# A two-layer encoder on one core: a third pair of split weight buffers, the attention bias masked by VectorE, and the softmax maximum kept with its sign turned

## The chip, the core and the metric

One core of a Trainium2 chip runs the whole program in one launch. The time is the device time in microseconds (us) of one execution; the medians are over several executions. Engines: PE is TensorE (matrix products), DVE is VectorE, ACT is ScalarE, POOL is GpSimd, SP is SyncE (it issues DMAs here). PEld is TensorE's weight load, which overlaps its products.

## The reference, cut to what is computed

Two layers on 256 rows of 1024, everything in float32. A layer is a mixer and a gated feed-forward.

```python
h = rms_norm(x, n1);  proj = h @ w_in_l                      # 1024 -> 2560
# a: 4 heads of neighbourhood attention, q and k normed per head, bias rpb per offset
s = einsum(q, k[idx]) * scale + bias;  out_a = softmax(s) @ v[idx]
# d: 6 heads, dilated windows (three patterns), partial rotary on q and k
# c: 6 query heads on 2 key/value heads, full attention, axial rotary on q and k
mix = concat(rms_norm(out_a), rms_norm(out_d), rms_norm(out_c))
x = x + mix @ w_out_l                                        # 1024 -> 1024
g, u = split(rms_norm(x, n2) @ w_gu)                         # 1024 -> 2 x 2816
g = conv3(g)                                                 # along the rows
x = x + (gelu(g) * u) @ w_dn                                 # 2816 -> 1024
```

## The kernel before, in words

**Products in split form.** A float32 weight is split into a high part (ScalarE rounds it, `wp_hi`) and a low part (VectorE subtracts, `wp_lo`), and so are the activations; each product is three faster ones (`mm3`). Weights come in units of up to 2048 columns for each of 128 partitions, in the order of use: `units_of` lists 18 for the mixer and then, for each of 11 feed-forward steps, a gate unit G, an up unit U and a down unit D. A unit lands in one of `RAWS` raw buffers, is split into one of `PARTS` pairs of buffers, and is used by TensorE. `unit()` asks, when unit i is wanted, for the loads up to i + AHEAD + RAWS - PARTS and for the splits up to i + AHEAD. Split instructions work on 384 to 1024 columns.

**Order.** Nothing is issued as written. `Plan` records each operation with what it must follow, and `order()` then gives each engine a fixed queue: again and again it takes the operation that can start earliest by its own costs (`cost`, and an estimate of a DMA's landing), with the place in the program (plus a shift, `later`) breaking ties. A buffer of a tag goes to tiles in the order of the program. Each engine then works through its queue in order, and waits where an operand is not there yet. An operation without operands to wait for may thus move far ahead of its place in the program.

**The mixer.** TensorE's projections and output projections are a filler (`Weave`) between the steps of the 16 heads: six of group d, six of c, four of a. For each two heads `scores` makes scores in PSUM (tile `psw`), `softens` does the softmax (VectorE the bias, the maximum `mx` and its negation `nm`; ScalarE the exponential and the scaling by `rs`), `turn` transposes and splits (`ch`, `cl`), `weigh` multiplies with the values. `prep_d`, `prep_c` and `prep_a` norm and rotate q and k (`z`, `sw`): the sums of squares come from ScalarE or VectorE, GpSimd makes their inverse roots (`small_ms`, `small_rstd`), VectorE or ScalarE scales. The rotation's tables (`cd`, `sd`, `cc`, `sc`, each for q and k) are GpSimd products of constants with a gain, made in `tables_d` and `tables_c` within the layer.

**The bias of group a.** `na_load` loads a few rows of `rpb`, `na_repeat` (GpSimd) scales them by 8 and copies them wide into `nab`, which goes to a scratch in DRAM; `na_diagonals` loads it back along diagonals, 448 KB in each of two DMAs; `na_bias_mask` (GpSimd, three additions of 576 columns) adds the mask. Layer 0 does this in its mixer; for layer 1 the three first steps stand in layer 0's feed-forward at the steps 2, 3 and 4 (`NA_STEPS`), and the mask in layer 1's mixer, but the order puts each where its operands and its buffer are first free: layer 1's copy runs at 110 us, its diagonal loads are issued at 121 us and its mask runs from 129 us, all at the end of layer 0's mixer. Layer 1's tables run at 32 to 57 us.

**From the mixer to the feed-forward.** The last output projections add to `xs` (`const_x`), ScalarE squares, TensorE transposes `xs`, ScalarE and VectorE scale and split it (`act_hT`), then G and U units follow.

The program's recording helper stands at line 393, so nearly every row of the profile has L393; the tiles' names tell the rows apart.

Of the kernel before, what the change touches and what calls it, by code (L numbers as in the profile page):

```python
# [11 lines left out]
F32 = mybir.dt.float32  # L12
# [6 lines left out]
P = 128  # L19
# [22 lines left out]
RAWS, PARTS, AHEAD, CHUNK = 4, 2, 2, 512  # L42
# [174 lines left out]
class Plan:  # L217
    def __init__(self, tc):
        self.tc, self.ops, self.shift, self.burst, self.bursts = tc, [], 0, None, {}
# [13 lines left out]
    @contextmanager  # L233
    def together(self):

        self.burst = len(self.bursts)
        self.bursts[self.burst] = []
        yield
        self.burst = None

    def add(self, engine, method, args, kw):
# [39 lines left out]
        for v in outs:  # L281
            v.tile.writes.append((i, v.footprint()))
        o.before.discard(i)
# [152 lines left out]
def encoder_kernel(  # L436
# [269 lines left out]
    def na_repeat(l):  # L706
        rows_ = nabs[l].rearrange("p r c -> p (r c)")[:NR]
        nc.gpsimd.tensor_scalar(nabs["few"], nabs["few"], ISCALE, None, ALU.mult)
# [7 lines left out]
    def na_diagonals(l):  # L716
        scr = nabs["scr"]
        for i in range(2):
# [3 lines left out]
            )  # L722

    load(0)
    for l in range(DEPTH):
# [81 lines left out]


        def tables_d(which, g):
            cd = act.tile([P, NT, HD], F32, tag=f"cd{which}", name=f"cd{which}{l}", bufs=1)  # L810
            sd = act.tile([P, NT, 16], F32, tag=f"sd{which}", name=f"sd{which}{l}", bufs=1)
            b = lambda v: v.unsqueeze(1).to_broadcast([P, NT, v.shape[1]])
            nc.gpsimd.tensor_tensor(cd, rot[:, :, 0:64], b(g[:, l, 1]), op=ALU.mult)
            for i in range(2):
                o, n = (8 * i, 8 * (1 - i)), 8
                nc.gpsimd.tensor_tensor(
                    sd[:, :, o[0] : o[0] + n],
                    rot[:, :, 64 + o[0] : 64 + o[0] + n],
                    b(g[:, l, 1, o[1] : o[1] + n]),
                    op=ALU.mult,  # L820
                )
            return cd, sd

        def tables_c(which, g):
            cc = act.tile([P, NT, HD], F32, tag=f"cc{which}", name=f"cc{which}{l}", bufs=1)
            sc = act.tile([P, NT, HD], F32, tag=f"sc{which}", name=f"sc{which}{l}", bufs=1)
            b = lambda v: v.unsqueeze(1).to_broadcast([P, NT, v.shape[1]])
            nc.gpsimd.tensor_tensor(cc, rot[:, :, 80:144], b(g[:, l, 2]), op=ALU.mult)
            for i in range(4):
                o, n = (16 * i, 16 * (i ^ 1)), 16  # L830
                nc.gpsimd.tensor_tensor(
                    sc[:, :, o[0] : o[0] + n],
# [544 lines left out]
```

## Time and profile before

| | |
|---|---|
| median of 3 executions | 625.4 us (625.36 to 627.85) |
| the profiled execution | 626.0 us, its span 624.2 us |
| PE busy | 608.7 us, 98% |
| DVE busy | 490.3 us, 79% |
| ACT busy | 430.6 us, 69% |
| POOL busy | 83.3 us, 13% |
| layer 0: mixer, feed-forward | about 0 to 126 us, 126 to 317 us |
| layer 1: mixer, feed-forward | about 317 to 432 us, 432 to 624 us |
| bytes moved | 104.66 MB, mean 168 GB/s |

Busy time is the union of an engine's instructions in the profile. A product's end is modelled, so a busy PE can still hide gaps of some tenths of a microsecond; where a row shows PE idle, it is. The clock granted to TensorE was full in all stages.

### The profile page before, as it was taken

How to read it: one execution, taken by the hardware profiler on the slowest of the kernel's cores; microseconds unless marked ns; L12 is line 12 of the kernel's file. 1: busy time of each engine (PE TensorE's matmuls, PEld its weight loads, DVE VectorE, ACT ScalarE, POOL GpSimd, SP SyncE). 2: the span in 40 equal slices, each digit the busy share in tenths (PEclk: the TensorE clock that was granted, in tenths of full speed). 3: DMA queues.
4: the chain of work that ended last, by engine and by line, in shares of the span. 5: the costliest groups of instructions: out<-in, count | busy, mean ns of one | idle time of the engine just before them, and what ended most of it. 6: DMA issues, size and time to landing. Idle time of an engine off the chain costs nothing.

```text
span 624.2 us, 9846 instructions
## 1 busy us (share of the span) xinstructions
PE 608.7 (98%) x3496; PEld 525.0 (84%) x3496; DVE 490.3 (79%) x1026; ACT 430.6 (69%) x1064; POOL 83.3 (13%) x131
## 2 busy tenths in 40 slices
PE   8999999989999999999999999998999999999997
PEld 6998888778888888888899979786888888888885
DVE  4889889798777777777867798978877777877775
ACT  6887998677655655565588799888765655566552
POOL 2764231340000000000023210312000000000000
PEclk9999999999999999999999999999999999999999
DMA  8794312866555555555444632043565655555511
GB/s 279 262 287 154 102 40 96 249 154 213 189 177 178 199 202 202 179 172 173 153 145 154 225 102 85 34 138 136 202 207 199 202 188 170 187 199 188 170 49 67
DMA packets 81345, 104.66 MB, mean 168 GB/s; under 512 B 9464, under 2 KB 68952, under 8 KB 81296
## 3 DMA queue, kind: packets, MB, share of 16 engines
q1 hardware_dynamic: 80720, 103.51, 51.0%
q8 instruction: 27, 0.44, 0.3%
q10 hardware_dynamic: 576, 0.53, 0.3%
q14 instruction: 22, 0.18, 0.1%
HBM read 102.54 MB, written 1.49 MB: 167 GB/s over the span
## 4 chain that ended last, share of the span: by engine, by line
PE 86%; ACT 4%; DVE 4%; DMA 3%; POOL 1%; issue 1%; SPq 0%; ACTq 0%; POOLq 0%; DVEq 0%
PE psw_w L393 47%; PE psa_a L393 39%; ACT act_s2k L393 2%; DMA act_nab<-dram_scr 1%; DVE wp_lo L393 1%; DMA dram_scr<-act_nab 1%; DVE act_s2k L393 1%; POOL small_rstd L393 1%; DVE act_hT L393 1%; DMA act_s2k<-in_norm_g_dram 1%; POOL act_nab L393 0%; ACT L393 0%; ACT wp_hi L393 0%; DVE const_x L393 0%; DVE act_z L393 0%
## 5 line engine op out<-in xcount | busy, mean ns | idle before, releaser
L393 DVE TENSOR_TENSOR wp_lo<-wp_raw,wp_hi 128x512 fp32r<-128x512 f32 (+2 forms) x348 | 248.3, 742 | 50.9 <-ACT wp_hi L393 49.1
L393 PE MATMUL psw_w<-act_hT,wp_hi 128*128 128x512 f32 x704 | 247.4, 396 | 4.7 <-DVE act_hT L393 4.7
L393 ACT CAST wp_hi<-wp_raw 128x512 fp32r<-128x512 f32 (+2 forms) x348 | 213.7, 658 | 25.1 <-PE psw_w L393 15.6
L393 PE MATMUL psw_w<-act_hT,wp_lo 128*128 128x256 f32 x704 | 195.7, 279 | 0.0
L393 PEld LDWEIGHTS psw_w<-act_hT,wp_hi 128*128 128x128 f32 x704 | 131.8, 188 | 36.8 <-DVE act_hT L393 5.9
L393 PEld LDWEIGHTS psw_w<-act_hT,wp_lo 128*128 128x128 f32 x704 | 132.6, 188 | 1.1
L393 PE MATMUL psa_a<-wp_hi,act_hT 128*128 128x384 f32 (+2 forms) x448 | 114.9, 335 | 0.0
L393 ACT COPY act_s2k<-psw_w 128x256 f32<-128x256 f32 x88 | 32.3, 372 | 81.1 <-PE psw_w L393 81.1
L393 PEld LDWEIGHTS psa_a<-wp_hi,act_hT 128*128 128x128 f32 x448 | 78.6, 190 | 2.3
L393 PE MATMUL psa_a<-wp_lo,act_hT 128*128 128x384 f32 (+2 forms) x224 | 74.6, 334 | 0.0
L393 PE MATMUL psa_a<-wp_lo,act_ch 128*128 128x512 f32 x176 | 69.5, 395 | 0.0
L393 PE MATMUL psa_a<-wp_hi,act_ch 128*128 128x512 f32 x176 | 69.4, 394 | 0.0
L393 PE MATMUL psa_a<-wp_hi,act_cl 128*128 128x512 f32 x176 | 66.2, 395 | 0.2 <-DVE act_cl L393 0.2
L393 DVE TENSOR_TENSOR act_s2k<-psw_w,act_s2k 128x256 f32<-128x256 f32 x88 | 36.8, 422 | 30.6 <-ACT act_s2k L393 30.0
L393 PEld LDWEIGHTS psa_a<-wp_lo,act_hT 128*128 128x128 f32 x224 | 42.5, 190 | 2.1 <-DVE wp_lo L393 1.0
L393 PEld LDWEIGHTS psa_a<-wp_hi,act_cl 128*128 128x128 f32 x176 | 33.2, 188 | 8.3 <-DVE act_cl L393 0.6
L393 PEld LDWEIGHTS psa_a<-wp_hi,act_ch 128*128 128x128 f32 x176 | 33.1, 188 | 7.7
L393 PEld LDWEIGHTS psa_a<-wp_lo,act_ch 128*128 128x128 f32 x176 | 33.1, 188 | 6.9
L393 DVE SCALAR_TENSOR_TENSOR act_s2k<-act_s2k,act_cw,act_s2k 128x255 f32<-128x255 f32 x88 | 36.7, 476 | 1.4 <-ACT act_s2k L393 1.3
L393 ACT ACTIVATE act_s2k<-act_s2k,act_cw 128x256 f32<-128x256 f32 x44 | 24.1, 595 | 13.3 <-DVE act_s2k L393 13.3
L393 POOL TENSOR_TENSOR small_rstd<-small_ms,const_mh 128x6 f32<-128x6 f32 (+2 forms) x26 | 31.3, 1203 | 2.1
L393 ACT ACTIVATE act_s2k<-act_s2k,small_rs 128x256 f32<-128x256 f32 x64 | 28.8, 506 | 3.3 <-DVE small_rs L393 3.3
(110 smaller groups left out, 764.0 us busy)
## 6 DMA issues: line engine op xcount, KB each, us to landing
wp_raw<-in_w_gate_up_dram SPq DMA_DIRECT2D x44, 1024.0 KB, 5.0
wp_raw<-in_w_down_dram SPq DMA_DIRECT2D x22, 1024.0 KB, 4.8
wp_raw<-in_w_in_dram SPq DMA_DIRECT2D x14, 768.0 KB, 4.8
wp_raw<-in_w_in_dram SPq DMA_DIRECT2D x8, 1024.0 KB, 5.5
wp_raw<-in_w_out_dram SPq DMA_DIRECT2D x8, 768.0 KB
wp_raw<-in_w_out_dram SPq DMA_DIRECT2D x4, 512.0 KB, 3.7
act_nab<-dram_scr SPq DMA_DIRECT2D x4, 448.0 KB, 6.7
out_dram<-const_x SPq DMA_DIRECT2D x4, 256.0 KB, 2.0
```

Of the source, the lines that this page charges most:

```text
L393: getattr(o.engine.real, o.method)(*map(real, o.args), **{k: real(v) for k, v in o.kw.items()})
```

## The change

Constants: three raw buffers for four, three split pairs for two, splits asked for three units ahead instead of two. The planner gets `not_before(engine)`: what is recorded inside follows, in the order, the last operation recorded so far for that engine. With it the three bias steps of layer 1 stand behind the last weight load asked for, and layer 1's rotation tables are made in layer 0's feed-forward at step 4, behind the last of the bias's GpSimd work. The bias's scaling on GpSimd goes; mask and scaling are one VectorE operation (`scalar_tensor_tensor`, three in a layer). In the softmax, a head with bias gets minus the score and its minimum, without bias the maximum with its sign turned; both write `nm` themselves, and the negation goes. For group c the score's scale moves into the gain of q (one more GpSimd operation a layer).

```diff
-RAWS, PARTS, AHEAD, CHUNK = 4, 2, 2, 512
+RAWS, PARTS, AHEAD, CHUNK = 3, 3, 3, 512
...
+    @contextmanager
+    def not_before(self, engine):
+        self.behind = max(i for i, o in enumerate(self.ops) if o.engine.name == engine)
+        yield
+        self.behind = None
...
+        if self.behind is not None:
+            o.before.add(self.behind)
...
     def na_repeat(l):
-        nc.gpsimd.tensor_scalar(nabs["few"], nabs["few"], ISCALE, None, ALU.mult)
...
+    def tables_c(l, which):
+        g = gains_of[which][:, l, 2]
+        if which == "q":
+            nc.gpsimd.tensor_scalar(g, g, SCALE, None, ALU.mult)
...
+    def tables_of(l):
+        for which in "qk":
+            tables["d" + which, l] = tables_d(l, which)
+        for which in "qk":
+            tables["c" + which, l] = tables_c(l, which)
...
                         nc.vector.tensor_tensor_reduce(
-                            sb[:, t], sps[t], bias[t], SCALE, -3e38, ALU.add, ALU.max, mx[:, t : t + 1]
+                            sb[:, t], sps[t], bias[t], -SCALE, 3e38, ALU.add, ALU.min, nm[:, t : t + 1]
                         )
-                    nc.vector.tensor_scalar_mul(nm, mx, -1.0)
                     for t in range(NT):
                         nc.scalar.activation(
-                            p[:, t], sb[:, t], AF.Exp, bias=nm[:, t : t + 1], accum_out=rs[:, t : t + 1]
+                            p[:, t], sb[:, t], AF.Exp, bias=nm[:, t : t + 1], scale=-1.0,
+                            accum_out=rs[:, t : t + 1],
                         )
                 else:
                     for t in range(NT):
-                        nc.vector.reduce_max(mx[:, t : t + 1], sps[t], axis=AX.X)
-                    nc.vector.tensor_scalar_mul(nm, mx, -SCALE)
+                        nc.vector.reduce_max(nm[:, t : t + 1], sps[t], axis=AX.X, negate=True)
...
         def na_bias_mask():
             for i in range(1, NR, 9):
                 nv = nabs[l][:, i : i + 9]
-                nc.gpsimd.tensor_tensor(
-                    nv, nv, na_mask.unsqueeze(1).to_broadcast([P, 9, GRID_W]), op=ALU.add
+                nc.vector.scalar_tensor_tensor(
+                    nv, nv, ISCALE, na_mask.unsqueeze(1).to_broadcast([P, 9, GRID_W]), ALU.mult, ALU.add
                 )
...
             if kind == "G" and l + 1 < DEPTH and s in NA_STEPS:
-                NA_STEPS[s](l + 1)
+                with nc.not_before("SP"):
+                    NA_STEPS[s](l + 1)
+            if kind == "G" and l + 1 < DEPTH and s == 4:
+                with nc.not_before("POOL"):
+                    tables_of(l + 1)
```

More of the change, by code (lines that the diff above doesn't have):

```diff
@@ L218, in __init__ @@
     def __init__(self, tc):
-        self.tc, self.ops, self.shift, self.burst, self.bursts = tc, [], 0, None, {}
+        self.tc, self.ops, self.shift, self.burst, self.bursts, self.behind = tc, [], 0, None, {}, None
         for name, short in (("tensor", "PE"), ("scalar", "ACT"), ("vector", "DVE"), ("gpsimd", "POOL"), ("sync", "SP")):
@@ L722, in na_diagonals, with tables_d @@
             )
+    def tables_d(l, which):
+        cd = act.tile([P, NT, HD], F32, tag=f"cd{which}", name=f"cd{which}{l}", bufs=1)
+        sd = act.tile([P, NT, 16], F32, tag=f"sd{which}", name=f"sd{which}{l}", bufs=1)
+        b = lambda v: v.unsqueeze(1).to_broadcast([P, NT, v.shape[1]])
+        nc.gpsimd.tensor_tensor(cd, gains_of["rot"][:, :, 0:64], b(gains_of[which][:, l, 1]), op=ALU.mult)
+        for i in range(2):
+            o, n = (8 * i, 8 * (1 - i)), 8
+            nc.gpsimd.tensor_tensor(
+                sd[:, :, o[0] : o[0] + n],
+                gains_of["rot"][:, :, 64 + o[0] : 64 + o[0] + n],
+                b(gains_of[which][:, l, 1, o[1] : o[1] + n]),
+                op=ALU.mult,
+            )
+        return cd, sd
+    def tables_c(l, which):
+        g = gains_of[which][:, l, 2]
+        if which == "q":
+            nc.gpsimd.tensor_scalar(g, g, SCALE, None, ALU.mult)
+        cc = act.tile([P, NT, HD], F32, tag=f"cc{which}", name=f"cc{which}{l}", bufs=1)
+        sc = act.tile([P, NT, HD], F32, tag=f"sc{which}", name=f"sc{which}{l}", bufs=1)
+        b = lambda v: v.unsqueeze(1).to_broadcast([P, NT, v.shape[1]])
+        nc.gpsimd.tensor_tensor(cc, gains_of["rot"][:, :, 80:144], b(g), op=ALU.mult)
+        for i in range(4):
+            o, n = (16 * i, 16 * (i ^ 1)), 16
+            nc.gpsimd.tensor_tensor(
+                sc[:, :, o[0] : o[0] + n],
+                gains_of["rot"][:, :, 144 + o[0] : 144 + o[0] + n],
+                b(g[:, o[1] : o[1] + n]),
+                op=ALU.mult,
+            )
+        return cc, sc
+    gains_of, tables = {}, {}
+    def tables_of(l):
[3 more added lines that the diff above has]
+            tables["c" + which, l] = tables_c(l, which)
     load(0)
@@ L806, in encoder_kernel @@
             gk = gk.rearrange("p (l a d) -> p l a d", l=DEPTH, d=HD)
[L809 to L815, printed above, removed]
-                nc.gpsimd.tensor_tensor(
[L817 to L832, printed above, removed]
-                    rot[:, :, 144 + o[0] : 144 + o[0] + n],
-                    b(g[:, l, 2, o[1] : o[1] + n]),
-                    op=ALU.mult,
-                )
-            return cc, sc
+            gains_of.update(q=gq, k=gk, rot=rot)
         def normed(ps, nh, t, name):
@@ L946, in softens @@
                 nm = small.tile([P, NT], F32, tag="nm", name=f"nm_{name}")
-                mx = small.tile([P, NT], F32, tag="mx", name=f"mx_{name}")
                 rs = small.tile([P, NT], F32, tag="rs", name=f"rs_{name}")
@@ L1030, in prep_d @@
         def prep_d(which, g):
-            cd, sd = tables_d(which, g)
+            if ("d" + which, l) not in tables:
+                tables["d" + which, l] = tables_d(l, which)
+            cd, sd = tables["d" + which, l]
             for t in range(NT):
@@ L1041, in prep_c @@
         def prep_c(which, g):
-            cc, sc = tables_c(which, g)
+            if ("c" + which, l) not in tables:
+                tables["c" + which, l] = tables_c(l, which)
+            cc, sc = tables["c" + which, l]
             nh = H_GQ if which == "q" else H_GKV
```

4 lines of the change are left out of this document (1 added, 3 removed).

## The prediction, made before the changed kernel ran

> **What bounds the kernel now.** I read the summary first, then busy time by stretches of 10 us, then TensorE's idle time and who ended it, then the order of time around those places.
>
> ```profile
> span 624.2 us, 9846 instructions
> PE 608.7 (98%) x3496; PEld 525.0 (84%) x3496; DVE 490.3 (79%) x1026; ACT 430.6 (69%) x1064; POOL 83.3 (13%) x131
> core 0: us, PE busy (x) PEld busy (x) DVE busy (x) ACT busy (x) POOL busy (x), PEclk, DMA share, GB/s
> 0.00:10.00 10.00, 7.89 (x34) 6.00 (x35) 3.15 (x8) 5.39 (x12) 2.76 (x11) 1.00 0.80 257
> 50.00:60.00 10.00, 8.88 (x64) 7.68 (x64) 10.00 (x30) 7.05 (x19) 4.93 (x7) 1.00 0.38 125
> 110.00:120.00 10.00, 8.69 (x47) 6.70 (x46) 8.23 (x17) 7.58 (x20) 4.08 (x4) 1.00 0.75 244
> 120.00:130.00 10.00, 9.66 (x53) 7.93 (x53) 8.40 (x17) 7.51 (x19) 2.06 (x4) 1.00 0.95 192
> 130.00:140.00 10.00, 8.06 (x50) 6.95 (x49) 10.00 (x16) 5.81 (x13) 5.95 (x6) 1.00 0.56 178
> 170.03:186.70 16.67, 16.67 (x90) 14.22 (x89) 12.51 (x22) 9.98 (x19) 0.00 (x0) 1.00 0.57 190
> 350.00:360.00 10.00, 9.51 (x76) 8.81 (x75) 5.64 (x24) 8.20 (x36) 3.20 (x4) 1.00 0.43 151
> 390.00:400.00 10.00, 9.17 (x55) 7.26 (x54) 9.59 (x25) 9.66 (x28) 4.53 (x5) 1.00 0.09 32
> 420.00:430.00 10.00, 9.45 (x51) 7.40 (x50) 7.84 (x16) 7.39 (x16) 1.95 (x3) 1.00 0.36 116
> 430.00:440.00 10.00, 7.18 (x43) 5.58 (x42) 9.64 (x19) 7.86 (x21) 1.85 (x3) 1.00 0.55 193
> 620.00:624.20 4.20, 0.48 (x3) 0.04 (x1) 0.75 (x1) 0.00 (x0) 0.00 (x0) 0.98 0.35 130
> ```
>
> TensorE is the bound: 608.7 of 624.2 us, at the full granted clock. The change takes no matmul away, so it can win back only the idle 15.5 us. Of these 2.1 lie in the first 10 us and 3.7 after 620 us (the last accumulation and the store), where it has nothing to say. That leaves 9.7 us: 1.1 in 50:60, 1.3 in 110:120, 0.3 and 1.9 in 120:140 (attention of layer 0 hands over to its feed-forward), 0.5, 0.8, 0.6 and 2.8 in the four stretches of layer 1, small change elsewhere. The feed-forward row (170:187) has TensorE busy throughout, with VectorE idle for 16.67 - 12.51 = 4.2 us of a step.
>
> Now the places themselves, in order of time; brackets give idle time and what ended it.
>
> ```profile
> 46.07 1.95 DVE L393 TENSOR_TENSOR wp_lo<-wp_raw,wp_hi 128x512 fp32r<-128x512 f32 x1 [1.27 <-ACT wp_hi L393]
> 51.33 1.42 POOL L393 TENSOR_TENSOR act_nab<-act_nab,const_na 128x576 f32<-128x576 f32 x1
> 51.45 1.72 DVE L393 TENSOR_TENSOR act_z<-act_z,act_ccq 128x384 f32<-128x384 f32 x1
> 53.17 0.14 DVE L393 TENSOR_SCALAR small_nm<-small_mx 128x2 f32<-128x2 f32 x1
> 53.28 0.91 ACT L393 ACTIVATE act_s2k<-act_s2k,small_rs 128x256 f32<-128x256 f32 x2 [2.48 <-DVE small_rs L393]
> 53.84 0.33 PE L393 MATMUL psw_w<-const_ident,act_s2k 128*128 128x128 f32 x1 [1.12 <-ACT act_s2k L393]
> 56.16 0.60 DVE L393 TENSOR_TENSOR act_z<-act_z,act_ccq 128x384 f32<-128x384 f32 x1
> 110.14 1.83 POOL L393 COPY act_nab<-act_few 28x1984 f32<-28x1984 f32 x1 [1.37 <-DVE small_ss L393]
> 110.74 1.26 DVE L393 TENSOR_SCALAR small_nm<-small_mx 128x2 f32<-128x2 f32 x1
> 122.36 1.32 ACT L393 CAST wp_hi<-wp_raw 128x512 fp32r<-128x512 f32 x2 [3.06 <-PE psa_a L393]
> 128.58 3.73 DVE L393 TENSOR_TENSOR wp_lo<-wp_raw,wp_hi 128x512 fp32r<-128x512 f32 x4
> 128.94 1.61 POOL L393 TENSOR_TENSOR act_nab<-act_nab,const_na 128x576 f32<-128x576 f32 x1 [6.58 <-DMA act_nab<-dram_scr]
> 132.23 1.65 DVE L393 SCALAR_TENSOR_TENSOR act_hT<-psw_w,const_gains,act_hT 128x256 fp32r<-128x256 f32 x4
> 187.44 1.89 DVE L393 TENSOR_TENSOR wp_lo<-wp_raw,wp_hi 128x512 fp32r<-128x512 f32 x3 [0.67 <-ACT wp_hi L393]
> 196.24 0.69 DVE L393 TENSOR_TENSOR act_cl<-act_s2k,act_ch 128x512 fp32r<-128x512 f32 x1 [0.21 <-ACT act_ch L393]
> 197.99 2.09 PE psa_a L393 x9
> 432.33 0.68 DVE L393 TENSOR_TENSOR wp_lo<-wp_raw,wp_hi 128x512 fp32r<-128x512 f32 x1
> 433.08 1.66 DVE L393 SCALAR_TENSOR_TENSOR act_hT<-psw_w,const_gains,act_hT 128x256 fp32r<-128x256 f32 x4
> ```
>
> The same VectorE instruction takes 0.60 us at 56.16 and 1.72 us at 51.45, where GpSimd works on the bias beside it; the 2-element negation takes 0.14 us, and 1.26 beside GpSimd's copy. Much of TensorE's idle time in layer 0 sits behind such stretched instructions.
>
> **The change part by part.** The other rows that the sum needs:
>
> ```profile
> L393 POOL TENSOR_TENSOR act_nab<-act_nab,const_na 128x576 f32<-128x576 f32 x6 | 9.1, 1534 | 12.6 <-DMA act_nab<-dram_scr 12.6
> L393 DVE TENSOR_SCALAR small_nm<-small_mx 128x2 f32<-128x2 f32 x32 | 6.5, 203 | 0.0
> L393 DVE SCALAR_TENSOR_TENSOR const_x<-psa_a,small_rstd,const_x 128x512 f32<-128x512 f32 x24 | 17.0, 742 | 3.6 <-POOL small_rstd L393 2.7 <-PE psa_a L393 1.0
> L393 DVE SCALAR_TENSOR_TENSOR act_mixT_lo<-psw_w,const_gains,act_mixT_hi 128x256 fp32r<-128x256 f32 x16 | 7.7, 478 | 1.6 <-ACT act_sqm L393 1.4
> 44.65 2.81 POOL L393 TENSOR_TENSOR act_nab<-act_nab,const_na 128x576 f32<-128x576 f32 x2 [6.03 <-DMA act_nab<-dram_scr]
> 32.05:38.65 6.60, 6.44 (x19) 1.00 1.09 348
> wp_raw<-in_w_gate_up_dram SPq DMA_DIRECT2D x44, 1024.0 KB, 5.0
> ```
>
> *Softmax negation.* All 32 go: 6.5 us of VectorE. On TensorE's path lie only those inside a chain that TensorE awaits. At 110.74 the instruction and the copy that stretched it both leave: 1.1 us, of which I take 0.9, since 110:120 has 1.3 idle. In layer 1's three stretches with 0.5 to 0.8 idle, 0.2 us each at most: 0.5. Minimum for maximum and a sign in the reduction change no shape; I cost them at nothing, as VectorE does the same elements.
>
> *Mask.* Three GpSimd additions of 1.5 us in each layer become three VectorE ones of 576 elements. From 742 ns for 512 and 478 for 256, an element is 1.03 ns, so about 0.81 us each, 2.4 us a layer (estimate). For layer 0 VectorE gets back what GpSimd took from it: 1.27 us at 46.07 (1.95 against 0.68 at 432.33) and 1.12 at 51.45, so its load stays even, but the stretch stands no longer between a head's sums and its scaling: gain 1.1 us, the idle time ahead of 53.84 (bounds 0 and 1.1). Layer 1's mask leaves the hand-over: four subtractions take 3.73 us at 128.58 where three take 1.89 at 187.44, so 1.2 us too long, and the activations TensorE awaits come right behind them at 132.23. The wait for the bias's DMA (6.03 and 6.58 us, idle GpSimd) moves onto VectorE's queue, where weight splits and softmax stand behind it. GpSimd reached its wait early because it had nothing else; VectorE has work up to 44.8 us, and the last transfer lands at 44.65. I take 0, with ends 0 and 6 us a layer.
>
> *Third pair, one raw buffer less.* A load of unit j used to wait for the split of j-4, that for TensorE's end with j-6; now it waits for the split of j-3, and that again for j-6. Loads start as before (5.0 us to landing against some 14 us until the split: three units of 5.6, a third of a step, less four subtractions at 0.63), so I cost the missing raw buffer at nothing; its cover is that lead. What changes is that a split may run one unit sooner. At 122.36 ScalarE had sat 3.06 us because no pair was free until TensorE ended an output projection; the first gate weights were split only then, and crowded the hand-over. With the 1.2 us above I take 1.7 of the 2.3 us idle in 120:140 (bounds 0 and 2.3), and in 430:440 the one subtraction ahead of 433.08: 0.7 of 2.8 (bounds 0 and 2.8). The wait for the activations themselves stays.
>
> *GpSimd and SyncE work moved into the feed-forward.* Layer 1's bias load, copy, scratch write and two diagonal loads, and its tables, now come at steps 2 to 4 of layer 0. The stretch at 32.05 has 6.44 us with one layer's tables, a product of gains (0.3) and one scaling of the bias (0.5), so about 5.6 us, and the copy 1.8. The scalings of the bias go; a scaling of one gain a layer comes, on the idle GpSimd. The loads are issued behind a weight load by the planner's order, so SyncE has 14 us of lead to lose 5 to 8 in. VectorE's cover is the 4.2 us a step, but the down projection's second operand ends at 196.93 and is used at 197.99: 1.06 us to spare. A copy stretching a VectorE instruction by 1.8 us costs 1.8 - 1.06 = 0.8; the tables, if they block for all of 5.6 us, 5.6 - 4.2 = 1.4, of which I take half; layer 1's mask, 2.4, fits into 4.2. Loss 1.5 us (bounds 0 and 5).
>
> [...]
>
> **Sum:** 0.9 + 0.5 + 1.1 + 1.7 + 0.7 - 1.5 = 3.4 us. The profiled execution took 626.0 us (1.8 around its span), so 622.6; the median before, 625.4, is 0.6 lower, so 622.0 us, 0.54% less.
>
> **The rivals.** *The feed-forward pays it back.* All 7.4 us of GpSimd count there: loss 3.2, and the gains keep only their contention part, 0.9 + 1.1 + 1.2 = 3.2: 625.4 us. For it: the 1.06 us to spare. Against: a further split pair takes urgency from the subtractions. *VectorE waits for the bias's DMA.* It reaches the mask early and stands, 6.0 us in layer 0 and 6.6 in layer 1: 625.4 - 4.9 + 12.6 = 633 in full; it makes the kernel slower by 0.5% once both waits pass 4.9 + 3.1 = 8 us. For it: the planner places an instruction by its own estimate of landing, and an in-order queue then waits. Against: VectorE has a backlog. *The third pair does nothing*, since the hand-over is a chain of latencies: 1.7 shrinks to 1.2, 0.7 to 0; 623.2 us. *Everything closes up*: all 9.7 us, 615.7.
>
> **How the numbers follow.** About 0.5% (3.1 us) is what a measurement of this kernel tells from no change. Forecast 0.45 (own range 619 to 624, of which about an eighth is above 622.3), everything closed up 0.06, feed-forward pays 0.25, third pair idle 0.10, VectorE waiting 0.14. Faster 0.46, same 0.40, slower 0.14. The range cuts the extremes of both sides: 617 to 628.
>
> **What would show it.** Right: no GpSimd work between layer 0's attention and step 2; no 1.7 us act_z or 1.2 us stretched subtraction; TensorE idle under 1 us in 120:140; SyncE never waiting on scratch. Wrong: VectorE's mask with a wait of several us on the diagonal loads; TensorE idle inside steps 2 to 6; a new wait at the start, where three loads instead of four are under way; or a reordered mixer whose heads wait where they did not.

## The result, and the profile after

The changed kernel takes 621.75 us, the median of four executions (621.14 to 622.49), against 625.73 us for the kernel before beside it (625.36 to 627.85): a ratio of 0.993, interval 0.9904 to 0.9956. The profiled execution took 621.45 us, its span is 619.7 us, 4.5 us shorter than before. 622.0 was predicted. The number is right. Most of the terms it was added up from are not.

The summary of the changed kernel (its helper stands at line 402, so rows carry L402):

```profile
span 619.7 us, 9851 instructions
PE 606.8 (98%) x3496; PEld 525.3 (85%) x3496; DVE 488.3 (79%) x1000; ACT 427.7 (69%) x1064; POOL 80.3 (13%) x125
```

TensorE's products are the same 3496, and its idle time is 619.7 - 606.8 = 12.9 us, 2.6 less than before. The other 1.9 us lie in its busy time, in which modelled ends can cover gaps. That the three products of the split form are each faster than one of float32 is measured here on transposes alone: in the changed kernel six float32 transposes of 128 columns take 0.82 us at 122.97, each 0.27 long, so they start some 0.11 us apart, 0.86 ns a column (an estimate from that row), where split products of 512 columns start 0.23 us apart, 0.45 ns a column. What a whole product in float32 would take no run shows. The stretches of 10 us, with the columns of the prediction's table:

```profile
50.00:60.00 10.00, 8.98 (x63) 7.52 (x62) 9.95 (x35) 9.00 (x25) 1.86 (x2) 1.00 0.13 50
110.00:120.00 10.00, 10.00 (x61) 8.68 (x61) 8.08 (x18) 7.99 (x20) 2.71 (x5) 1.00 0.36 122
120.00:130.00 10.00, 8.87 (x49) 6.83 (x47) 9.17 (x18) 8.83 (x22) 2.60 (x4) 1.00 0.44 148
130.00:140.00 10.00, 9.99 (x58) 8.81 (x59) 9.19 (x18) 6.69 (x13) 0.36 (x1) 1.00 0.86 291
140.00:150.00 10.00, 9.46 (x47) 7.47 (x46) 8.74 (x16) 7.02 (x14) 8.71 (x12) 1.00 0.37 127
390.00:400.00 10.00, 10.00 (x71) 8.61 (x70) 9.35 (x24) 8.41 (x24) 1.26 (x2) 1.00 0.15 52
430.00:440.00 10.00, 8.99 (x56) 7.83 (x55) 9.19 (x17) 5.95 (x13) 2.34 (x3) 1.00 0.62 202
```

In 110:120 the 1.3 us of idle are gone, in 120:140 they fall from 2.3 to 1.1, in 50:60 they stay, and in 140:150, where the moved GpSimd work fills 8.71 us, 0.5 stand where 0.2 stood. In layer 1 the 0.8 of 390:400 are gone and the 2.8 of 430:440 are 1.0, with another 1.1 now just ahead of it (the row at 428.63 below). Single places, in order of time:

```profile
52.03 0.33 PE L402 MATMUL psw_w<-const_ident,act_s2k 128*128 128x128 f32 x1 [1.02 <-ACT act_s2k L402]
130.01 0.50 PE L402 MATMUL psw_w<-act_hT,wp_hi 128*128 128x512 f32 x1 [1.01 <-DVE act_hT L402]
141.21 1.84 POOL L402 COPY act_nab<-act_few 28x1984 f32<-28x1984 f32 x1 [10.85 <-DMA act_few<-in_rpb_dram]
142.60 1.00 DVE L402 TENSOR_TENSOR wp_lo<-wp_raw,wp_hi 128x512 fp32r<-128x512 f32 x1
143.52 0.94 DVE L402 TENSOR_TENSOR act_s2k<-act_s2k,act_s2k 128x512 f32<-128x512 f32 x1
144.50 0.62 ACT L402 CAST act_ch<-act_s2k 128x512 fp32r<-128x512 f32 x1 [1.53 <-DVE act_s2k L402]
145.17 0.50 PE L402 MATMUL psa_a<-wp_hi,act_ch 128*128 128x512 f32 x1 [0.54 <-ACT act_ch L402]
428.63 0.50 PE L402 MATMUL psw_w<-act_hT,wp_hi 128*128 128x512 f32 x1 [1.11 <-DVE act_hT L402]
```

Where the time came from, by the start of the same products in the two traces: the first gate product of layer 0 is 1.83 us earlier (126.89 to 125.06), the second half of that gate unit 2.74 (132.75 to 130.01), the first down product 1.81, the end of layer 0 2.27. So 0.9 us of the gain are lost again by the first down product. There VectorE does a weight subtraction (142.60), stretched to 1.00 us beside the copy of the bias, ahead of the operation that the product's operand waits for (143.52). Layer 1 gains as much again: its first gate product is 4.99 us earlier (433.62 to 428.63), its end 4.54.

### The profile page after: what moved, and what is told of

Read it like the earlier page. It is cut to its first block, busy times and chain, and to the rows that moved or that the text cites. A ratio compares the mean times of both kernels' runs of the same rounds, so it can differ in the third digit from the quotient of the medians.

```text
span 619.7 us, 9851 instructions
## 1 busy us (share of the span) xinstructions
PE 606.8 (98%) x3496; PEld 525.3 (85%) x3496; DVE 488.3 (79%) x1000; ACT 427.7 (69%) x1064; POOL 80.3 (13%) x125
## 3 DMA queue, kind: packets, MB, share of 16 engines
HBM read 102.54 MB, written 1.49 MB: 168 GB/s over the span
## 4 chain that ended last, share of the span: by engine, by line
PE 86%; ACT 5%; DVE 3%; DMA 3%; issue 1%; POOL 1%; ACTq 0%; DVEq 0%
PE psw_w L402 49%; PE psa_a L402 37%; DMA wp_raw<-in_w_in_dram 2%; ACT act_s2k L402 2%; DVE wp_lo L402 1%; ACT wp_hi L402 1%; DMA const_x<-in_x_dram 1%; DVE const_x L402 1%; ACT act_z L402 0%; POOL small_rstd L402 0%; DVE act_hT L402 0%; DVE small_nm L402 0%; ACT act_hT L402 0%; DVE act_s2k L402 0%; ACT act_ch L402 0%
## 5 line engine op out<-in xcount | busy, mean ns | idle before, releaser
L402 DVE TENSOR_TENSOR wp_lo<-wp_raw,wp_hi 128x512 fp32r<-128x512 f32 (+2 forms) x348 | 246.3, 734 | 42.4 <-ACT wp_hi L402 39.3
L402 PE MATMUL psw_w<-act_hT,wp_hi 128*128 128x512 f32 x704 | 247.5, 396 | 3.2 <-DVE act_hT L402 3.1
L402 ACT CAST wp_hi<-wp_raw 128x512 fp32r<-128x512 f32 (+2 forms) x348 | 212.8, 662 | 37.6 <-issue 22.0
L402 PE MATMUL psw_w<-act_hT,wp_lo 128*128 128x256 f32 x704 | 195.8, 279 | 0.0
L402 PEld LDWEIGHTS psw_w<-act_hT,wp_hi 128*128 128x128 f32 x704 | 131.8, 188 | 35.5 <-DVE act_hT L402 4.5
L402 PEld LDWEIGHTS psw_w<-act_hT,wp_lo 128*128 128x128 f32 x704 | 132.6, 188 | 1.1
L402 PE MATMUL psa_a<-wp_hi,act_hT 128*128 128x384 f32 (+2 forms) x448 | 114.3, 333 | 0.0
L402 ACT COPY act_s2k<-psw_w 128x256 f32<-128x256 f32 x88 | 32.4, 372 | 85.3 <-PE psw_w L402 85.3
L402 PEld LDWEIGHTS psa_a<-wp_hi,act_hT 128*128 128x128 f32 x448 | 78.4, 189 | 3.1 <-ACT act_s2k L402 0.3
L402 PE MATMUL psa_a<-wp_lo,act_hT 128*128 128x384 f32 (+2 forms) x224 | 74.8, 334 | 0.0
L402 PE MATMUL psa_a<-wp_hi,act_ch 128*128 128x512 f32 x176 | 69.6, 395 | 0.5 <-ACT act_ch L402 0.5
L402 PE MATMUL psa_a<-wp_lo,act_ch 128*128 128x512 f32 x176 | 69.4, 394 | 0.0
L402 PE MATMUL psa_a<-wp_hi,act_cl 128*128 128x512 f32 x176 | 69.1, 395 | 0.0
L402 DVE TENSOR_TENSOR act_s2k<-psw_w,act_s2k 128x256 f32<-128x256 f32 x88 | 36.9, 423 | 38.3 <-ACT act_s2k L402 37.3
L402 PEld LDWEIGHTS psa_a<-wp_lo,act_hT 128*128 128x128 f32 x224 | 42.5, 190 | 0.9
L402 PEld LDWEIGHTS psa_a<-wp_hi,act_ch 128*128 128x128 f32 x176 | 33.2, 188 | 8.7 <-ACT act_ch L402 1.1
L402 PEld LDWEIGHTS psa_a<-wp_hi,act_cl 128*128 128x128 f32 x176 | 33.2, 188 | 8.1 <-DVE act_cl L402 0.4
L402 DVE SCALAR_TENSOR_TENSOR act_s2k<-act_s2k,act_cw,act_s2k 128x255 f32<-128x255 f32 x88 | 37.2, 481 | 2.8 <-ACT act_s2k L402 2.8
L402 PEld LDWEIGHTS psa_a<-wp_lo,act_ch 128*128 128x128 f32 x176 | 33.2, 188 | 6.9
L402 ACT ACTIVATE act_s2k<-act_s2k,act_cw 128x256 f32<-128x256 f32 x44 | 24.1, 595 | 16.1 <-DVE act_s2k L402 16.1
L402 POOL TENSOR_TENSOR small_rstd<-small_ms,const_mh 128x6 f32<-128x6 f32 (+2 forms) x26 | 31.8, 1222 | 2.2
L402 PE MATMUL psw_w<-act_ch,const_v 128*128 128x256 f32 x128 | 28.5, 286 | 0.6 <-ACT act_s2k L402 0.6
```

Of the source, the lines that this page charges most:

```text
L402: getattr(o.engine.real, o.method)(*map(real, o.args), **{k: real(v) for k, v in o.kw.items()})
```

## The experiments

Twelve kernels, each timed beside the kernel before on the same chip. I cut the change into four parts (*pair*: the constants 3, 3, 3; *softmax*: `nm` written by the reduction; *mask*: the VectorE operation; *move*: bias steps and tables into the feed-forward), ran each alone, then the changed kernel without each. Layer 0 is the time from the span's start to the first projection product of layer 1, layer 1 the time from there to the last down product, both in the profiled execution. "Full clock" is the median of those executions whose mean granted clock was at least 0.999, with their number. Ratios are to the kernel before on the same chip, whose median was 625.73 to 626.48.

Two things disturb the columns of layers, which come from one execution each. TensorE is slower at the start: in the kernel before, products of 384 columns start 0.32 us apart at 8.35 us and 0.17 at 11.81, though the granted clock is given as 1.00 for 8 to 10 us and for 11 to 12 us alike. The profiled executions differ early: the 61st projection product starts at 21.29 us in the kernel before, at 22.31 with softmax alone, 22.65 with the pair alone and 20.55 with the mask alone, so layer 0 can differ by 1 us and more by its start only. And the granted clock drops to half for 3.4 us twice in the executions shown of pair alone and move alone (layer 0 twice; layers 0 and 1), and once in those of mask alone and all but softmax (layer 1); the one of a negation for each row tile holds one as well, by its mean clock of 0.997 (an estimate). A drop costs about 1.6 us, as worked out under the move.

| kernel | median | ratio, interval | full clock | layer 0 | layer 1 |
|---|---|---|---|---|---|
| before (beside the four single parts) | 626.12 | 1 | 625.56 (21 of 31) | 316.95 | 303.13 |
| changed | 621.75 | 0.9930 [0.9904, 0.9956] | 621.30 (2 of 4) | 314.68 | 300.86 |
| pair alone | 629.14 | 1.0044 [1.0022, 1.0066] | 626.84 (3 of 10) | 323.12 | 303.18 |
| softmax alone | 623.60 | 0.9953 [0.9938, 0.9969] | 623.53 (9 of 10) | 319.40 | 299.74 |
| mask alone | 625.59 | 0.9997 [0.9978, 1.0016] | 623.99 (1 of 10) | 314.58 | 304.82 |
| move alone | 627.88 | 1.0030 [1.0014, 1.0046] | 626.48 (1 of 10) | 317.69 | 305.02 |
| all but the pair | 618.64 | 0.9890 [0.9860, 0.9920] | 618.64 (4 of 4) | 312.75 | 299.68 |
| all but softmax | 627.88 | 1.0026 [1.0006, 1.0045] | none of 10 | 316.13 | 304.63 |
| all but the mask | 620.38 | 0.9919 [0.9895, 0.9942] | 620.05 (3 of 4) | 313.56 | 300.57 |
| all but the move | 621.14 | 0.9931 [0.9908, 0.9954] | 621.13 (4 of 4) | 314.72 | 300.82 |
| a negation for each row tile | 623.29 | 0.9952 [0.9935, 0.9969] | 623.26 (5 of 6) | 317.96 | 299.26 |
| softmax, exponentials held | 619.25 | 0.9888 [0.9863, 0.9912] | 619.25 (4 of 4) | 315.88 | 298.21 |
| pair, splits asked later | 621.50 | 0.9924 [0.9901, 0.9947] | 621.50 (4 of 4) | 316.51 | 299.00 |
| softmax and mask | 619.44 | 0.9882 [0.9852, 0.9912] | 619.44 (4 of 4) | 314.11 | 299.68 |

**The pair alone.**

```diff
-RAWS, PARTS, AHEAD, CHUNK = 4, 2, 2, 512
+RAWS, PARTS, AHEAD, CHUNK = 3, 3, 3, 512
```

> The kernel before with three split pairs, three raw buffers and splits asked for three units ahead; nothing else of the change. Terms add up: the third pair is worth 0.5 us in 120:140 and 0.7 us in 430:440, all at the two hand-overs from attention to feed-forward, so 624.5 us, with the contention beside the mask and beside the copy still there. Rival, the pair is the main thing: 3 us or more, since half of the change's 4 us lies in layer 1, where of the moved work only tables and the mask are missing. Rival, the queues are dealt anew: gain or loss of 1 to 2 us at places that have nothing to do with free pairs.

It is slower, by 0.44%; at full clock by 1.3 us. The order of time around its worst place:

```profile
43.98 5.05 POOL L402 TENSOR_TENSOR act_nab<-act_nab,const_na 128x576 f32<-128x576 f32 x3 [4.67 <-DMA act_nab<-dram_scr]
46.37 1.66 ACT L402 CAST wp_hi<-wp_raw 128x512 fp32r<-128x512 f32 x3 [4.61 <-DMA wp_raw<-in_w_in_dram]
56.31 0.47 PE L402 MATMUL psw_w<-const_ident,act_s2k 128*128 128x128 f32 x1 [2.13 <-ACT act_s2k L402]
```

And the stretch behind it (columns as in the tables of stretches):

```profile
56.19:59.60 3.41, 3.29 (x12) 3.00 (x13) 3.41 (x12) 2.95 (x10) 2.99 (x5) 0.50 0.00 0
```

GpSimd stands 4.67 us for the bias (6.03 in the kernel before) and ScalarE 4.61 for weights that have not landed, TensorE waits 2.13 us for the first head, and then runs 3.41 us at half clock. This profiled execution is the longest of the ten and has two such drops in layer 0, so of its 6.2 us longer layer 0 some 3.2 are the two drops, an estimate, and 1.4 the start.

**Softmax alone.** The softmax hunks of the change and nothing else (negation gone, `nm` from the reduction).

> The kernel before with the softmax maximum kept with its sign turned (no negation, the scale of group c in the gain of q); nothing else. Terms add up: VectorE loses 32 instructions and 6.5 us, TensorE's path 0.2 us at three or four places: 624.8 us; the stretched instruction beside the copy at 110 us is then another one. Rival, the pair is the main thing: no change, 625.4. Rival, the queues are dealt anew: 1 to 2 us either way.

Faster by 0.47%; layer 1 is 3.4 us shorter, and layer 0, with the same instructions taken out, 2.5 us longer, of which 1.0 is the start. The rest was not foreseen and comes back below.

**Mask alone.**

```diff
-                nc.gpsimd.tensor_tensor(nv, nv, na_mask..., op=ALU.add)
+                nc.vector.scalar_tensor_tensor(nv, nv, ISCALE, na_mask..., ALU.mult, ALU.add)
```

> The kernel before with mask and scaling of the bias as one VectorE operation; nothing else. Terms add up: 1.1 us at 52 us and 1.2 us at 129 us are won back from contention: 623.1 us, and VectorE has a wait of under 1 us on the diagonal loads. Rival, VectorE waits for the bias's DMA: 3 to 6 us of waiting in its queue at about 40 us or at 125 us, 627 us or more. Rival, the queues are dealt anew: 1 to 2 us either way, and TensorE's wait of 1.1 us at 54 us is still there.

No change of the whole that the interval tells from none. The trace shows a gain and a loss. Four rows (the last with the columns of the stretches):

```profile
49.66 0.56 DVE L402 TENSOR_TENSOR act_z<-act_z,act_ccq 128x384 f32<-128x384 f32 x1
127.75 2.48 DVE L402 TENSOR_TENSOR wp_lo<-wp_raw,wp_hi 128x512 fp32r<-128x512 f32 x4
131.01 0.50 PE L402 MATMUL psw_w<-act_hT,wp_hi 128*128 128x512 f32 x1 [1.01 <-DVE act_hT L402]
431.48:434.90 3.42, 3.42 (x11) 2.94 (x12) 3.42 (x8) 2.84 (x8) 1.85 (x3) 0.50 0.01 3
```

Without GpSimd beside it `act_z` takes 0.56 us for 1.72, and TensorE no longer waits ahead of the first head, where it stood 1.12 us. The four subtractions at the hand-over take 2.48 us for 3.73, and the wait ahead of the gate's second half falls from 1.94 to 1.01. Layer 0 is 2.4 us shorter, 0.7 of it by the start. Layer 1 is 1.7 us longer, and there the clock drops at 431.48. Nine of the ten executions fell short of full clock, 21 of 31 of the kernel before kept it; where the clock dropped in those not profiled is not recorded. VectorE waits once for the bias's DMA:

```profile
DVE act_nab L402 <- DMA act_nab<-dram_scr: 1.0, 1, 1.0
```

(wait, us in all, times, longest.) So the rival in which VectorE stands for 6 us a layer is out, and in the changed kernel no such wait is left.

**Move alone.**

```diff
-                NA_STEPS[s](l + 1)
+                with nc.not_before("SP"):
+                    NA_STEPS[s](l + 1)
+            if kind == "G" and l + 1 < DEPTH and s == 4:
+                with nc.not_before("POOL"):
+                    tables_of(l + 1)
```

> The kernel before with layer 1's three bias steps and its tables moved into layer 0's feed-forward; nothing else (mask on GpSimd, negation kept, two pairs). Terms add up: 0.9 us at 110 us and 1.2 us at 129 us won, 1.5 us lost in the feed-forward with two pairs: 624.8 us. By full blocking beside GpSimd the loss is 3.2 us: 626.5 us. Rival, the queues are dealt anew: 1 to 2 us either way.

Slower by 0.30%, and its profile shows what can make up most of that, at the hand-over of layer 1 (stretches, then the row of the order of time that ends the pause):

```profile
430.00:435.38 5.38, 3.56 (x19) 2.45 (x18) 4.71 (x10) 5.12 (x15) 0.75 (x1) 1.00 0.70 245
435.38:438.80 3.42, 3.42 (x12) 2.90 (x11) 3.42 (x7) 2.26 (x7) 1.85 (x3) 0.50 0.14 38
```

```profile
434.72 0.50 PE L402 MATMUL psw_w<-act_hT,wp_hi 128*128 128x512 f32 x1 [1.59 <-DVE act_hT L402]
```

The eighth column is the granted clock: 0.50 for 3.4 us. Products of 512 columns start 0.43 us apart there and 0.23 elsewhere, so 3.41 x (1 - 0.23/0.43) = 1.6 us are lost. The same happens at layer 0's hand-over, from 128.18.

**All but one part.** From the changed kernel, each part undone by the reverse of its diff.

> The changed kernel with two split pairs, four raw buffers and splits two units ahead again; all else of the change kept. If the parts add up as measured alone (pair +2.8 us, softmax -2.9, mask -0.2, move +1.9), it is faster than the changed kernel by 2.8: about 619 us. If the third pair pays only where the bias and the tables are out of its way, it is slower than the changed kernel: the prediction's own terms for the pair (0.5 and 0.7 us at the hand-overs, and 0.7 of cover in the feed-forward) give 623.5 us. If the queues are merely dealt anew, anything within 2 us of 622, with idle time at other places.

> The changed kernel with the negation kept (and the scale of group c in the exponential); all else of the change kept. If the parts add up as measured alone, 621.8 + 2.9 = 624.7 us, the dearest of the four. By the prediction's term 0.5 to 1.4 us: 623. If the queues are dealt anew, within 2 us of 622.

> The changed kernel with the bias scaled and masked by GpSimd again; all else of the change kept. As measured alone: no change, 622 us. By the prediction's term: 1.1 us at about 52 us come back, 622.9, and the mask of layer 1 now stands in the feed-forward, where GpSimd is beside 4.2 us of idle VectorE a step: 0 to 1 us more. [...]

> The changed kernel with layer 1's bias steps and tables left where the order puts them (in layer 0's mixer); all else of the change kept. As measured alone, the move costs 1.9 us, so this is faster than the changed kernel: 620 us. By the prediction's terms it is slower by 0.9 + 1.2 at the hand-over and faster by 1.5 in the feed-forward: 622.4 us. If the third pair pays only with the move, much slower: over 625 us.

Without the pair the kernel is faster than with it: 617.49 to 619.30 us in four executions, all below the 621.14 to 622.49 of the changed kernel. Without softmax it is slower than the kernel before. Without the move it is what it was. Without the mask its four executions are lower too, 619.71 to 620.93. But the changed kernel was timed apart from these four, and the intervals of all three ratios overlap with its own, that without the pair the least (0.9860 to 0.9920 against 0.9904 to 0.9956), so the 1.4 us of the mask are not settled. The parts do not add: alone they come to 0.44 - 0.47 - 0.03 + 0.30 = +0.24%, together they make -0.70%. Part of that can be the clock: with the softmax part TensorE's pause before layer 1's gate is short (a table below), and 32 of the 34 executions of the experiments that have it kept full clock; without it (pair, mask, move alone, all but softmax) 5 of 40 did. The split is not clean: the kernel before kept it in 21 of 31, the changed kernel in 2 of 4.

**Two ways to take the softmax part to pieces**, both on the kernel before. One keeps a negation but gives each row tile its own, 64 in all for 32:

```diff
                     for t in range(NT):
-                        nc.vector.reduce_max(mx[:, t : t + 1], sps[t], axis=AX.X)
-                    nc.vector.tensor_scalar_mul(nm, mx, -SCALE)
+                        nc.vector.reduce_max(mx[:, t : t + 1], sps[t], axis=AX.X)
+                        nc.vector.tensor_scalar_mul(nm[:, t : t + 1], mx[:, t : t + 1], -SCALE)
```

> The kernel before with one change: the softmax negation is done for each row tile by itself, right after its maximum, 64 small VectorE instructions in place of 32. Measured so far: with the negation gone, layer 1 is 3.4 us shorter, and a head's first exponential starts 0.8 to 1.0 us after its first maximum instead of 1.9 to 2.3. If the gain is the earlier start (one negation for both tiles makes the first exponential wait for the second maximum), this one keeps most of it though VectorE has more to do: start about 1.2 us after the maximum, layer 1 at 300 to 301 us of 303.1, whole 624. If the gain is VectorE's saved instructions, this one is slower than before by up to 3 us.

With twice the negations it is as fast as with none: 0.9952, and layer 1 takes 299.26 us against 299.74. So what the softmax part brings is not the instructions that it saves. The other has the softmax part, but takes the second row tile's maximum first and records both exponentials behind the last VectorE operation, so that none starts before the two maxima:

```diff
-                    for t in range(NT):
+                    for t in reversed(range(NT)):
                         nc.vector.reduce_max(nm[:, t : t + 1], sps[t], axis=AX.X, negate=True)
                     for t in range(NT):
-                        nc.scalar.activation(p[:, t], sps[t], AF.Exp, ...)
+                        with nc.not_before("DVE"):
+                            nc.scalar.activation(p[:, t], sps[t], AF.Exp, ...)
```

> The kernel before with the softmax part alone (no negation), but the second row tile's maximum is taken first and both exponentials are held until the other one is done: VectorE saves the same instructions, the first exponential starts as late as the second maximum allows. If the gain is the earlier start, it is mostly gone: layer 1 at 302 us or more, whole 625 us. If it is VectorE's saved instructions, as without the hold: layer 1 at 299.7, whole 623.6.

It is faster still, 0.9888. The hold puts the first exponential at a median of 1.26 us (layer 0) and 1.34 us (layer 1) behind the start of the first maximum; the kernel before has 1.72 and 2.24, softmax alone 0.79 and 0.99, a negation for each tile 1.30 and 1.13. This is neither of the two outcomes expected. With the hold the first exponential waits for the second maximum as before, and layer 1 is the shortest of all, so that wait is not the price; and the kernel with 64 negations says that VectorE's saved instructions are not. What both have, against the kernel before, is no negation of both tiles between maxima and exponentials, and a start under 1.4 us in layer 1. That a start below this brings nothing more fits, but is argued. Why this kernel's layer 0 is 3.5 us shorter than that of softmax alone, 1.2 of it by the start, is not settled: the instructions are the same, the order differs.

What the shared negation cost is to be read in one pair of heads of layer 1, in order of time, VectorE and ScalarE. The kernel before:

```profile
364.57 0.41 DVE L393 CUSTOM_DVE_ANT_0 act_s2k<-psw_w,const_dil 128x256 f32<-128x256 f32 x1
364.91 0.42 DVE L393 CUSTOM_DVE_ANT_0 act_s2k<-psw_w,const_dil 128x256 f32<-128x256 f32 x1
365.52 0.15 DVE L393 TENSOR_SCALAR small_nm<-small_mx 128x2 f32<-128x2 f32 x1
366.06 0.51 ACT L393 ACTIVATE act_s2k<-act_s2k,small_nm 128x256 f32<-128x256 f32 x1
366.62 0.42 DVE L393 CUSTOM_DVE_ANT_0 act_s2k<-psw_w,const_dil 128x256 f32<-128x256 f32 x1
367.52 0.16 DVE L393 TENSOR_SCALAR small_nm<-small_mx 128x2 f32<-128x2 f32 x1
368.19 0.90 ACT L393 ACTIVATE act_s2k<-act_s2k,small_rs 128x256 f32<-128x256 f32 x2
368.99 0.50 ACT L393 ACTIVATE act_s2k<-act_s2k,small_nm 128x256 f32<-128x256 f32 x1
370.55 0.91 ACT L393 ACTIVATE act_s2k<-act_s2k,small_rs 128x256 f32<-128x256 f32 x2
```

Softmax alone:

```profile
366.37 0.43 DVE L402 CUSTOM_DVE_ANT_0 act_s2k<-psw_w,const_dil 128x256 f32<-128x256 f32 x1 [0.27 <-PE psw_w L402]
367.34 0.51 ACT L402 ACTIVATE act_s2k<-act_s2k,small_nm 128x256 f32<-128x256 f32 x1
367.67 0.42 DVE L402 CUSTOM_DVE_ANT_0 act_s2k<-psw_w,const_dil 128x256 f32<-128x256 f32 x1
368.83 0.50 ACT L402 ACTIVATE act_s2k<-act_s2k,small_nm 128x256 f32<-128x256 f32 x1
369.32 1.70 ACT L402 ACTIVATE act_s2k<-act_s2k,small_rs 128x256 f32<-128x256 f32 x4
```

Before, the first exponential starts 366.06 - 364.57 = 1.49 us after the first maximum, since the negation needs both maxima and stands behind other VectorE work. The second head's negation starts 0.48 us after its maxima end (367.52 against 367.04), behind a reciprocal and another tile's operation, and its exponential then stands behind the first head's scaling on ScalarE: 2.4 us from 366.62 to 368.99. From the first maximum to the end of the last scaling it is 371.46 - 364.57 = 6.9 us before and 371.02 - 366.37 = 4.65 with softmax alone, where the four exponentials run one after the other and one group of scalings follows. The median over layer 1's eight pairs goes from 7.15 to 4.95 us.

Where TensorE gets the time back shows in all fourteen kernels alike, in layer 1. For each, the start of the last product with the values (the end of the heads' work on TensorE) behind the start of the layer, how many of the layer's 96 output products (those of the output projection, 0.23 us each) are still to come then, and the time from the start of the last output product to the first gate product:

| kernels | negation for both tiles | split pairs | last values, us | output products left | to the gate, us |
|---|---|---|---|---|---|
| before; mask alone; move alone | yes | 2 | 108.4 to 108.8 | 19 | 3.44; 3.45; 3.45 |
| pair alone; all but softmax | yes | 3 | 108.1 | 14 | 3.67; 3.65 |
| softmax alone; all but pair; softmax and mask | no | 2 | 104.2 to 104.3 | 29 | 0.36; 0.36; 0.35 |
| a negation for each row tile | no | 2 | 103.4 | 35 | 0.23 |
| softmax, exponentials held | no | 2 | 102.8 | 31 | 0.23 |
| changed; all but mask; all but move | no | 3 | 105.0 to 105.1 | 26 | 1.59 each |
| pair, splits asked later | no | 3 | 102.9 | 28 | 1.06 |

Without the shared negation the heads are done 3 to 6 us earlier, more output products are left behind them, and these cover the chain that makes the activations of the gate. Of softmax alone's 3.4 us in layer 1, 3.1 are this hand-over, 1.0 lies ahead of it, and 0.7 is lost again in the feed-forward. In layer 0 softmax alone goes the other way: the last values come at 122.05 us (118.23 before), 18 output products are left (24 before), and the way to the gate is 2.97 us long (0.59 before). Why the heads of layer 0 come late there is not settled.

**The pair's price.** With one raw buffer less, loads are asked for up to unit i + 3 instead of i + 4. ScalarE's waits for a mixer weight to land (us in all, times, longest), in the kernel before:

```profile
ACT wp_hi L393 <- DMA wp_raw<-in_w_in_dram: 1.3, 1, 1.3
```

The changed kernel:

```profile
ACT wp_hi L402 <- DMA wp_raw<-in_w_in_dram: 5.2, 6, 1.7
```

All but the pair:

```profile
ACT wp_hi L402 <- DMA wp_raw<-in_w_in_dram: 1.4, 1, 1.4
```

The pair with splits asked later:

```profile
ACT wp_hi L402 <- DMA wp_raw<-in_w_in_dram: 5.1, 4, 1.7
```

The last one tries whether the pair does harm because its splits are asked for earlier and so stand ahead of the heads' work in the order:

```diff
-RAWS, PARTS, AHEAD, CHUNK = 3, 3, 3, 512
+RAWS, PARTS, AHEAD, CHUNK = 3, 3, 2, 512
```

> The changed kernel with its three pairs and three raw buffers, but splits asked for two units ahead as before. The asking only sets the rank of a split among the operations that are ready in the planner; the buffers are the changed kernel's. If the third pair's price (3.1 us) comes from splits that now rank ahead of the heads' work on ScalarE and VectorE, it is won back: 619 to 620 us. If it comes from the one raw buffer less (ScalarE waits 5.2 us in all for weights to land, 1.4 with four), it stays: 621.5.

Half yes. Layer 1 comes back from 300.86 to 299.00, where the kernel without the pair has 299.68. Layer 0 goes the other way, from 314.68 to 316.51 against 312.75. The waits for weights stay at 5.1 us.

In layer 0 the time follows the lead of the loads (312.75 with i + 4, 314.68 with i + 3, 316.51 with i + 2), but the traces do not make the missing raw buffer the cause. All waits of ScalarE for a weight that last over 0.25 us are over by 45 us. In the kernel with splits asked later the last output product of layer 0 nevertheless starts at 122.75 us, earlier than without the pair (123.73); its loss lies behind that, 3.72 us to the first gate product for 0.36, and 1.4 us in the feed-forward. The changed kernel loses, against all but the pair, 0.8 us up to the last output product of layer 0, 0.2 from there to the gate and 1.0 in the feed-forward; in layer 1 0.2, then 1.2 at the hand-over (the table above), and the feed-forward gives 0.2 back. Three pairs with four raw buffers, which would separate the buffer from the pair, were not tried.

One place shows what the third pair does to the order, here with the pair alone, where no GpSimd work is near:

```profile
152.06 0.68 DVE L402 TENSOR_TENSOR wp_lo<-wp_raw,wp_hi 128x512 fp32r<-128x512 f32 x1
154.04 0.50 PE L402 MATMUL psa_a<-wp_hi,act_ch 128*128 128x512 f32 x1 [0.94 <-ACT act_ch L402]
```

A weight subtraction stands ahead of the VectorE operation (at 152.65) that the operand of the first down product waits for, and TensorE stands 0.94 us. In the kernel before that operation comes first (145.35), and TensorE does not wait.

**Softmax and mask** are all that the best kernel needs:

> The kernel before with the softmax part and the mask on VectorE; two pairs, and layer 1's bias and tables left in layer 0's mixer. Softmax, mask and move together made 618.6 us; the move alone cost 1.9, and nothing beside the third pair. If the move is worth nothing, 618.5 us, and these two edits are the change. If the hand-over of layer 0, where the softmax part alone lost 2.4 us, needs the bias's copy and DMA out of its way, 621 us or more.

0.9882, as good as all but the pair (0.9890). Both beat the kernel before and the changed one. The mask brings 4 us on top of softmax alone (623.60 to 619.44), and 0.5 us without it. By the layers it is all in layer 0 (319.40 to 314.11, 0.8 of it by the start), where softmax alone had lost 2.5 us. These 4 us need not be the mask's own: with the exponentials held, softmax alone comes to 619.25 without it. Which instruction there is late is not settled.

## Why the prediction was right in its number and wrong in its terms

- *Softmax, 0.9 + 0.5 us.* The step that failed is "in layer 1's three stretches with 0.5 to 0.8 idle, 0.2 us each at most". It priced an instruction by its length. The runs show 3.4 us in layer 1 (303.13 to 299.74), and the same with twice the negations. The bound by TensorE's idle time failed with it: I let the softmax win only from the 1.9 us of three stretches, and gave the 2.8 us of the hand-over to a chain of its own. It was none. From the start of the last output product to the first gate product it takes 3.44 to 3.67 us in all five kernels that keep the shared negation and 0.23 to 1.59 in all nine without: the heads come earlier, so their last projections cover the activations' chain. That leaving the shared negation does this is shown; which link of the heads' chain makes it, the one operation for two tiles or the place that the next one loses on ScalarE, is read from one pair of heads and stays open. At 110 us the forecast 1.3 us of idle are gone, but with the negation kept (all but softmax) they are gone too, and with softmax alone 1.2 stay: this was the copy's leaving.
- *Mask, 1.1 us (and the 1.2 us at the hand-over).* Right by itself in place and nearly in size: with the mask alone the wait of 1.12 us ahead of the first head is gone and that ahead of the gate's second half is 0.93 us shorter. In the whole time this does not show, and the clock can hide it: nine of ten executions fell short of full clock, and the one that kept it took 623.99 us against 625.56. In the changed kernel TensorE waits 1.02 us ahead of the first head again (the row at 52.03), though GpSimd no longer adds the mask and `act_z` there takes 0.55 us. Of the kernels with the mask on VectorE none of the three with two pairs has a wait there, and two of the four with three pairs do (1.02 and 0.71 us); by what it comes back is not settled. The two other estimates held:

```profile
L402 DVE SCALAR_TENSOR_TENSOR act_nab<-act_nab,const_na x6: 736/751/753, 39.5 to 189.5; 128x576 f32<-128x576 f32 x6
```

  six operations of 0.75 us (least, median and most, in ns) where 0.81 was worked out, and no wait for the bias's DMA.
- *Third pair, 0.5 of the 1.7 us at layer 0's hand-over, and 0.7.* Wrong in sign: without it the kernel is some 3 us faster. "I cost the missing raw buffer at nothing; its cover is that lead" rested on a lead measured in the feed-forward; in the mixer ScalarE did wait for weights (5.2 us for 1.3). But most of the price, as far as the traces show, is paid elsewhere, 1.2 us at layer 1's hand-over and 1.0 in layer 0's feed-forward. That a split "may run one unit sooner" was taken for a gain only: it also puts a subtraction ahead of what TensorE waits for (152.06 with the pair alone). How the price divides between the buffer and the order stays open. The fall of layer 1's hand-over from 3.44 to 1.59 us came with the softmax: without the pair it is 0.36.
- *Feed-forward, -1.5 us.* The mechanism was right in part. Beside GpSimd's copy (1.84 us from 141.21) the subtraction at 142.60 took 1.00 us, for 0.68 at 432.33 before, and beside its first products for the tables (0.90 us from 143.02) the operation at 143.52 took 0.94, for 0.69 at 145.35 before; TensorE stood 0.54 us, and 0.9 us were lost by the first down product. It needs the third pair's order as well: with the pair alone TensorE stands 0.94 us at the same product with nothing stretched, and with two pairs and the move (all but the pair) it does not stand there at all. It happened in step 1, not at steps 2 to 4, as the order took the operations forward. The rival's 3.2 us was the author's estimate: 5.6 us of tables and 1.8 of copy, 7.4 in all, less the 4.2 us that VectorE is idle in a step. That all of it blocks VectorE is not shown: the two stretched rows are 0.32 and 0.25 us too long, and the time lost behind them is 0.9. Over the whole kernel the move costs nothing measurable (0.9930 with, 0.9931 without), so what it cost here it gave elsewhere, or it was covered.
- *The rivals.* "The third pair does nothing" was nearest for that part and still too kind; VectorE waiting for the bias did not occur. SyncE did wait for the scratch, 3.2 us in two waits, with nothing late behind it.

The term that I took too large (the pair) and the one too small (softmax) cancelled to 0.3 us. That was luck. A total that comes out is no evidence for its parts.

## What to carry to other kernels

Price a small instruction by the chain that it closes, not by its length, and look for the gain where TensorE runs out of other work: here at the hand-over, by how many independent products are left when the chain ends. A buffer more, which lets work run sooner, can also let it run ahead of what is waited for. Where a planner deals the queues, undo each part of a change in company of the others: here a part that looked harmless (the pair) cost some 3 us of the gain, and a new deal of the queues moved a layer by some 2 us. Look at the clock of a part measured alone: a drop of 1.6 us can hide a gain such as the mask's.

## What the hardware showed that I had not expected

TensorE's granted clock falls to 0.50 for 3.41 us at a time, behind pauses that are shorter than that. In the kernel with the move alone nothing but eight transposes ran between an output projection's start at 431.27 and the first gate product at 434.72, 3.45 us with two pauses of 0.22 and 1.59; the clock fell at 435.38. In the kernel with the pair alone it fell at 56.19, in a pause of 2.13 us, and at 124.46, behind two of 0.55 and 1.01.

The falls of one execution lie whole multiples of 3.413 us apart: 68.27 us with the pair alone (20 times), 307.20 with the move alone (90 times), and 191.14 with the mask alone (56 times), counted there to the fall at the program's end. So I lay a grid of stretches of 3.41 us over an execution from one such fall; that it runs through the whole execution rests on these three distances alone. The profile says how long TensorE was busy in each stretch. Two stretches of the pair alone and one of the move alone, then two of the kernel before, whose grid is laid from the fall at its end, 624.02 (columns as above, TensorE first):

```profile
52.78:56.19 3.41, 1.40 (x12) 1.19 (x10) 3.29 (x17) 2.09 (x8) 0.99 (x1) 1.00 0.37 141
121.05:124.46 3.41, 1.86 (x9) 1.38 (x10) 3.41 (x7) 2.60 (x6) 0.73 (x1) 1.00 0.55 156
431.97:435.38 3.41, 1.59 (x10) 1.24 (x10) 3.34 (x8) 3.41 (x12) 0.00 (x0) 1.00 0.52 202
```

```profile
429.46:432.87 3.41, 2.35 (x13) 1.41 (x11) 3.18 (x5) 3.16 (x9) 0.19 (x1) 1.00 0.81 300
129.09:132.50 3.41, 1.73 (x14) 1.40 (x12) 3.41 (x5) 3.40 (x9) 3.24 (x4) 1.00 0.10 17
```

Over the fourteen profiled executions there are 2487 stretches between 3 and 610 us. Behind seven of them the clock fell; in these TensorE was busy for 1.40 to 1.86 us. Of all others only one had so little, the last row. In the kernel before the next lowest is 2.29 us, in the changed kernel the lowest is 2.27, and the clock stayed at 1.00. So in these traces the falls go with a stretch of the grid in which TensorE is busy for 1.86 us of 3.41 or less, not with the length of a pause alone; why the last row had no fall is not shown. The hand-over of the kernel before is as long as that of the move alone, 3.44 us, but a border of its grid at 432.87 divides it: TensorE is busy for 2.35 us of the stretch before it and 2.66 of the one behind, and the clock stayed. Of the kernel before 21 of 31 executions kept full clock (median 625.56 us), ten did not (627.62); that their grid lay otherwise fits, but only the profiled execution shows its grid. So a pause can cost its length and then some 1.6 us more (the estimate under the move), and a change that shortens it can gain both. Whether the transposes count as work is not told apart by these rows.
